# FFN up projections of a two-layer backbone block: seven block products in place of eight, with the activation through DRAM

## The chip, the cores and the metric

The kernel runs on 1 core of one Trainium2 chip. The metric is device microseconds of one execution. The kernel before takes 2263.75 us (median of 3 runs, 2263.47 to 2264.12). The names of the engines are those of the profile: PE is TensorE's matmul, PEld its weight load, DVE is VectorE, ACT is ScalarE, POOL is GpSimd, SP is SyncE, which here issues the DMAs.

## The reference, cut to what matters

1024 tokens of 1024 features go through two layers. Layer 0 has a pooling and attention mixer, layer 1 a token-gating mixer; behind each mixer stands the same FFN, with its own weights (D_FF is 2816, float32 throughout):

```python
def conv_ffn(h, w_up, conv_w, conv_b, w_down):
    hu = h @ w_up                                  # (1024, 1024) @ (1024, 5632)
    hcv = lax.conv_general_dilated(hu, conv_w[:, None, :], window_strides=(1,), padding='SAME',
                                   dimension_numbers=('NWC', 'WIO', 'NWC'),
                                   feature_group_count=hu.shape[-1]) + conv_b
    gate, up = jnp.split(hcv, 2, axis=-1)
    return (jax.nn.silu(gate) * up) @ w_down       # (1024, 2816) @ (2816, 1024)

x = post(x, mixer(pre(x, ...)), g_mix_post, gt_m)      # x + gate * rmsnorm(y)
x = post(x, conv_ffn(pre(x, ...), ...), g_ffn_post, gt_f)
```

The convolution runs over the tokens, three wide, separately for each of the 5632 features.

## The kernel before

**Products.** A float32 matrix is held as the sum of two float32r parts, `hi` (ACT casts it, line 115 for weights) and `lo` (DVE subtracts `hi` from the float32 value, line 52). `three` (lines 121 to 123) forms a product of two such matrices from three matmuls of 128 x 128 by 128 x 512 (hi hi, hi lo, lo hi). `piece` loads 128 x 512 weights (256 KB), casts and subtracts; its tiles come from the pool `wp`, open for the whole program, with 4 raw buffers, so the weights of the next stage can be loaded while the last one still runs.

**Up phase of the FFN.** The features stand on the partitions. There are 44 chunks of 128 output features: chunk f (0 to 21) of the gate and chunk 22 + f of the up half. Each chunk is worked for two halves of 512 tokens (`h[0]`, `h[1]`), over 8 blocks of 128 input features: 44 x 2 x 8 x 3 = 2112 matmuls in a layer. The modulated input of half 1 isn't ready when the phase begins: the mixer's last projection (tiles `e` in layer 0, `o` in layer 1) has just ended, and `tail` (`post`, then `post_pair` for two pairs of token blocks) has to norm it, add the residual, norm again, transpose on PE (tiles `tra`, `trb`) and modulate. So `ffn_order` runs the first 6 chunks (HEAD = 3 pairs) for half 0 alone, then for half 1, and the others for both. Names: `hiha`, `loha` are half 0's input in layer 0, `hihb` and so on those of half 1, `hiu`, `lou` a chunk's weights, `pu` the PSUM bank.

**Activation.** `conv_unit` applies the convolution to the 512 tokens of a bank: ACT's Identity with scale and bias (line 366), two DVE instructions over 511 columns (`stt`, line 49), and some one-column instructions for the seam between the halves. `gated` multiplies. Half 0's activation is split and stays on the chip; half 1's goes to DRAM (`act_d`, 256 KB for each f).

**Down phase.** 22 blocks of the contraction, half by half, 1056 matmuls in a layer (tiles `d`, weights `rawd`, `hid`, `lod`); half 1's activation is read back (`arw`). `post` of the result makes the input of the next mixer (tiles `sv` are its first projection).

**Background.** `ada_block` computes 512 modulation columns: 4 DMAs of 512 KB, 8 DVE instructions of 128 x 512 (`aacc`), a few small ones. Six blocks run in layer 0's up phase, two in layer 1's.

**Order.** A tile framework assigns buffers from pools, adds the semaphore waits, and sets each engine's order by priorities (`tc.high_priority` moves the weights' loads and splits ahead). Each engine runs its instructions in order. A pool that opens where another has closed takes over its space, and waits until the last reader is done.

The listing shows the kernel before, with the lines that the profile names.

## Time and profile before

| | |
|---|---|
| runs of the kernel before | 2263.47, 2263.75, 2264.12 us |
| span of the profiled execution | 2260.8 us |
| span of layer 0's up phase (482.9 to 970.3) | 487.40 us |
| span of layer 1's up phase (1520.3 to 2004.0) | 483.70 us |
| PE busy | 2222.1 us, 98% of the span |
| DVE, ACT, POOL busy | 1336.0, 958.1, 0.2 us |

The profiler gives the span, from the first to the last recorded instruction of one execution; that execution's own device time isn't listed apart from it. The median of the runs is 2.95 us above the span, and this difference is taken as what lies around the span. The mean duration of a matmul of 128 x 512 in the groups is its time from issue to end; neighbours overlap, so what one costs is the distance between two starts. The same holds for DVE: the starts of two neighbours lie a little closer than one lasts.

### The profile page before, as it was taken

Reading aid. Unit: us, or ns where it says so; the run is one execution under the profiler, and the core shown is the slowest. Engines: PE = TensorE matmul, PEld = TensorE weight load, DVE = VectorE, ACT = ScalarE, POOL = GpSimd, SP = SyncE. Lnnn points to the kernel's source line nnn. Section 1 sums busy time; section 2 is a strip of 40 time slices with the busy share of each in tenths; the row PEclk is TensorE's granted clock in tenths of the full one; section 3 lists DMA queues with packets and bytes.
Section 4 is the critical chain, followed back from the end, with each engine's and each line's share of the span. In section 5 each row is a group of like instructions: output and inputs, shape, how many; then the busy total and the mean of one; then the engine's idle time right before and its main releaser. Section 6 shows DMA issues by size and latency. Waiting matters only on the chain.

```text
span 2260.8 us, 27374 instructions
## 1 busy us (share of the span) xinstructions
PE 2222.1 (98%) x9862; PEld 1744.5 (77%) x9862; DVE 1336.0 (59%) x2608; ACT 958.1 (42%) x1766; POOL 0.2 (0%) x4
## 2 busy tenths in 40 slices
PE   6999999999999999999999999999999999999998
PEld 3775455888888888888887888878888888888776
DVE  5686667678875455534625467379655555443555
ACT  5645654465333333324524432266333333323444
POOL 0000000000000000000000000000000000000000
PEclk9999999999999999999999999999999999999999
DMA  8110112554451111225535246246411111124675
GB/s 305 63 43 19 52 47 92 189 200 145 159 168 65 61 61 57 66 89 164 178 97 168 93 132 195 88 166 205 140 65 61 60 63 61 61 80 131 197 246 181
DMA packets 120824, 266.25 MB, mean 118 GB/s; under 512 B 13416, under 2 KB 14056, under 8 KB 120560
## 3 DMA queue, kind: packets, MB, share of 16 engines
q1 hardware_dynamic: 120688, 264.51, 35.9%
q8 instruction: 77, 1.26, 0.2%
q14 instruction: 59, 0.48, 0.1%
HBM read 236.14 MB, written 28.31 MB: 117 GB/s over the span
## 4 chain that ended last, share of the span: by engine, by line
PE 92%; DMA 3%; DVE 2%; ACT 1%; issue 1%; SPq 0%; DVEq 0%; ACTq 0%
PE pu L121 15%; PE pu L122 15%; PE pu L123 15%; PE d L122 6%; PE d L121 6%; PE d L123 6%; PE o L710 3%; PE tr L703 2%; PE o L122 1%; PE o L121 1%; PE sv L121 1%; PE o L123 1%; PE sv L123 1%; PE sv L122 1%; DMA rawd<-in_wdn_dram 1%; PE e L121 1%
## 5 line engine op out<-in xcount | busy, mean ns | idle before, releaser
L49 DVE SCALAR_TENSOR_TENSOR c<-pu,cvw,c 128x511 f32<-128x511 f32 x352 | 263.3, 749 | 214.9 <-ACT c L366 209.7
L52 DVE TENSOR_TENSOR lod<-rawd,hid 128x512 fp32r<-128x512 f32 x220 | 151.5, 691 | 254.7 <-ACT hid L115 252.0
L121 PE MATMUL pu<-hiha,hiu 128*128 128x512 f32 x704 | 274.4, 390 | 0.0
L122 PE MATMUL pu<-loha,hiu 128*128 128x512 f32 x704 | 274.2, 389 | 0.0
L122 PE MATMUL pu<-lohb,hiu 128*128 128x512 f32 x704 | 274.1, 389 | 0.0
L123 PE MATMUL pu<-hiha,lou 128*128 128x512 f32 x704 | 274.1, 389 | 0.0
L123 PE MATMUL pu<-hihb,lou 128*128 128x512 f32 x704 | 274.1, 389 | 0.0
L121 PE MATMUL pu<-hihb,hiu 128*128 128x512 f32 x704 | 274.0, 389 | 0.0
L115 ACT CAST hid<-rawd 128x512 fp32r<-128x512 f32 x220 | 136.6, 622 | 286.8 <-PE d L123 239.7
L115 ACT CAST hiu<-rawu 128x512 fp32r<-128x512 f32 x208 | 129.5, 623 | 283.5 <-PE pu L122 256.2
L52 DVE TENSOR_TENSOR lou<-rawu,hiu 128x512 fp32r<-128x512 f32 x208 | 143.5, 690 | 147.5 <-ACT hiu L115 146.7
L366 ACT ACTIVATE c<-pu,cvw 128x512 f32<-128x512 f32 x176 | 136.5, 777 | 142.8 <-PE pu L123 142.8
L122 PE MATMUL d<-lod,a 128*128 128x512 f32 x448 | 177.8, 397 | 1.3 <-DVE lod L52 1.2
L123 PE MATMUL d<-hid,a 128*128 128x512 f32 x448 | 176.9, 395 | 0.0
L121 PE MATMUL d<-hid,a 128*128 128x512 f32 x448 | 176.6, 396 | 0.0
L123 PEld LDWEIGHTS pu<-hihb,lou 128*128 128x128 f32 x704 | 132.2, 188 | 27.4
L123 PEld LDWEIGHTS pu<-hiha,lou 128*128 128x128 f32 x704 | 132.2, 188 | 27.4
L121 PEld LDWEIGHTS pu<-hihb,hiu 128*128 128x128 f32 x704 | 132.2, 188 | 27.3
L122 PEld LDWEIGHTS pu<-loha,hiu 128*128 128x128 f32 x704 | 132.2, 188 | 27.3
L122 PEld LDWEIGHTS pu<-lohb,hiu 128*128 128x128 f32 x704 | 132.2, 188 | 27.2
L121 PEld LDWEIGHTS pu<-hiha,hiu 128*128 128x128 f32 x704 | 132.2, 188 | 27.1
L49 DVE SCALAR_TENSOR_TENSOR aacc<-ar,silc,aacc 128x512 f32<-128x512 f32 x140 | 104.7, 748 | 15.1 <-DMA ar<-in_wada_b_dram 13.7
(355 smaller groups left out, 3851.2 us busy)
## 6 DMA issues: line engine op xcount, KB each, us to landing
rawd<-in_wdn_dram SPq DMA_DIRECT2D x220, 256.0 KB, 2.7
rawu<-in_wup_dram SPq DMA_DIRECT2D x200, 256.0 KB, 2.6
ar<-in_wada_b_dram SPq DMA_DIRECT2D x80, 512.0 KB, 3.9
actd<-c SPq DMA_DIRECT2D x44, 256.0 KB, 2.0
arw<-actd SPq DMA_DIRECT2D x44, 256.0 KB, 2.9
aw<-in_wada_a_dram SPq DMA_DIRECT2D x16, 512.0 KB, 7.1
rawe<-in_wout_e_dram SPq DMA_DIRECT2D x32, 256.0 KB, 3.0
rawsv<-in_win_v_dram SPq DMA_DIRECT2D x32, 256.0 KB, 2.6
```

The costliest lines, as they stand in the source:

```text
L49: V.scalar_tensor_tensor(out=out, in0=in0, scalar=scalar, in1=in1, op0=op0, op1=op1)
L52: V.tensor_tensor(out=out, in0=in0, in1=in1, op=op)
L115: A.copy(out=hi, in_=raw)
L121: nc.tensor.matmul(ps, a[0], b[0], start=first, stop=False)
L122: nc.tensor.matmul(ps, a[0], b[1], start=False, stop=False)
L123: nc.tensor.matmul(ps, a[1], b[0], start=False, stop=last)
L366: A.activation(out=c, in_=ps, func=AF.Identity, scale=w1, bias=b)
L703: nc.tensor.transpose(out=tr[:, j * P:(j + 1) * P], in_=pr[j][:, c * P:(c + 1) * P], identity=ident)
L710: nc.tensor.matmul(po, vv[:, kb, a], pt, start=c == 0, stop=c == nch - 1)
```

## The change

Take one f. Its gate and up chunks (128 output features each), the two halves of the input features (blocks 0 to 3 and 4 to 7) and the two halves of the tokens form a 2 x 2 by 2 x 2 block product: A11, A12 are the gate chunk's weights for the two halves of the input features, A21, A22 those of the up chunk; B11, B21 are token half 0's input features, B12, B22 those of token half 1. The kernel before does 8 block products, of 12 matmuls each. The changed one does 7, with sums on both sides (Winograd's form of Strassen's scheme):

- weight sums, anew for every f: s1 = A21 + A22, s2 = s1 - A11, s3 = A11 - A21, s4 = A12 - s2 (DVE, 128 x 512 each, float32);
- input sums, once in a layer: t1 = B12 - B11, t2 = B22 - t1, t3 = B22 - B12, t4 = B21 - t2, made by `post_sums` in 8 steps (2 pairs of token blocks, 4 steps `kk` of two feature blocks); in a step ACT runs 7 instructions of 128 x 256, DVE 7, POOL 4;
- products: `stage_a` does A11 B11 (into `x`) and A12 B21 (`y`), `stage_b` s2 t2 (added to `x`), s1 t1 (`z`) and s3 t3 (added to `x`), `stage_c` s4 B22 (added to `z`) and A22 t4 (added to `x`). Between them x, y and z are copied and added into two tiles of 1024 tokens, `c1` (gate) and `c2` (up).

Each of the seven left-hand sides is split into hi and lo (7 ACT casts, 7 DVE subtractions of 128 x 512). The convolution then runs on `c1` and `c2` in SBUF, over 1024 columns at once, without a seam. The whole activation (512 KB for each f) goes to DRAM, and the down phase reads back both halves (`load_acts(0)`, `load_acts(1)`). `stage_a` of the first three f (LEAD = 3), which need half 0 alone, run while half 1 is made. The pool of the weights is now opened and closed by stage: `wp0` (layer 0's mixer), none in an up phase, whose own pool `up0` or `up1` holds its weights, `wd0` (down), `wn0` (layer 1's mixer), `wd1`.

The core of the diff (removed lines that the listing shows are left out, as are the changes to comments):

```diff
-    wp = ctx.enter_context(tc.tile_pool(name="wp", bufs=3))
...
+    def open_wp(es, name):
+        pools["wp"] = es.enter_context(tc.tile_pool(name=name, bufs=3))
...
+    def post_sums(ys, step, nxt, name, h0, b22, ts):
+        l, w = nxt
+        y = ys[0]
+        for pair in range(2):
+            post_pair(y, 1, pair, ys[1], step, None, nxt, f"{name}{pair}", False)
+            tsl = slice(2 * pair * P, 2 * (pair + 1) * P)
+            for kk in range(4):
+                nm = f"{name}{pair}{kk}"
+                ps = bank(f"tr{nm}")
+                for q in range(2):
+                    for i in range(2):
+                        nc.tensor.transpose(out=ps[:, (2 * q + i) * P:(2 * q + i + 1) * P],
+                                            in_=y[:, 2 * pair + i, (kk + 4 * q) * P:(kk + 4 * q + 1) * P],
+                                            identity=ident)
+                full, ta, tb = ntmp("fs" + nm), ntmp("ta" + nm), ntmp("tb" + nm)
+                W = 2 * P
+                for q in range(2):
+                    k = kk + 4 * q
+                    A.activation(out=full[:, q * W:(q + 1) * W], in_=ps[:, q * W:(q + 1) * W], func=AF.Identity,
+                                 scale=gmod[:, l, w, k:k + 1], bias=ada[:, l, 24 * w + k:24 * w + k + 1])
+                b12, f22 = full[:, 0:W], full[:, W:2 * W]
+                t = [ta[:, 0:W], ta[:, W:2 * W], tb[:, 0:W], tb[:, W:2 * W]]
+                h0h, h0l = (x.bitcast(F32) for x in h0)
+                A.copy(out=b22[:, 0, kk, tsl], in_=f22)
+                tt(t[0], b12, h0h[:, kk, tsl], ALU.subtract)
+                tt(t[0], t[0], h0l[:, kk, tsl], ALU.subtract)
+                G.tensor_tensor(out=t[2], in0=f22, in1=b12, op=ALU.subtract)
+                G.tensor_tensor(out=t[1], in0=f22, in1=t[0], op=ALU.subtract)
+                tt(b22[:, 1, kk, tsl], f22, b22.bitcast(F32)[:, 0, kk, tsl], ALU.subtract)
+                tt(t[3], h0h[:, kk + 4, tsl], t[1], ALU.subtract)
+                tt(t[3], t[3], h0l[:, kk + 4, tsl], ALU.add)
+                for i in (0, 2, 1, 3):
+                    A.copy(out=ts[i][:, 0, kk, tsl], in_=t[i])
+                    (G.tensor_tensor if i in (1, 2) else V.tensor_tensor)(
+                        out=ts[i][:, 1, kk, tsl], in0=t[i], in1=ts[i].bitcast(F32)[:, 0, kk, tsl], op=ALU.subtract)
+    LEAD = 3
+    def ffn(l, pu, h0, tail, step, nxt, background=()):
...
+        act_d = dram.tile([NF, P, T], F32, name=f"actd{l}")
...
+            def split(src, name):
+                t = up.tile([P, 2, HT], F32R, tag="hl", name=name, bufs=4)
                 A.copy(out=t[:, 0, :], in_=src)
                 tt(t[:, 1, :], src, t.bitcast(F32)[:, 0, :], ALU.subtract)
+                return t
+            def product(ps, w, b, first):
+                for k in range(4):
+                    ks = slice(k * P, (k + 1) * P)
+                    three(ps, (w[:, 0, ks], w[:, 1, ks]), b(k), first and k == 0, k == 3, not first)
+            def raw_sum(f, name, in0, in1, op):
+                s = up.tile([P, HT], F32, tag="s", name=f"{name}_{l}_{f}", bufs=4)
+                tt(s, in0, in1, op)
+                return s
+            def c_tile(name):
+                return up.tile([P, T], F32, tag="c", name=name, bufs=6)
...
+                o = 2 * (f % 2)
...
+                with tc.high_priority():
+                    for i in range(2):
+                        nc.sync.dma_start(out=ring[f][i], in_=wup[l, f + i * NF])
+            def stage_a(f):
+                nm = f"{l}_{f}"
+                ws = []
+                if f >= LEAD:
+                    load(f)
+                for i in range(2):
+                    with tc.high_priority():
+                        if f >= LEAD:
+                            raw = ring[f][0][:, halves(i)]
+                        else:
+                            raw = up.tile([P, HT], F32, tag="ra", name=f"ra{nm}_{i}", bufs=2)
+                            nc.sync.dma_start(out=raw, in_=wup[l, f][:, halves(i)])
+                        ws.append(split(raw, f"wa{nm}_{i}"))
+                x = chain[f] = pu(f"x{nm}")
+                c1 = c1s[f] = c_tile(f"c1{nm}")
+                product(x, ws[0], lambda k: (h0[0][:, k, :], h0[1][:, k, :]), True)
+                A.copy(out=c1[:, 0:HT], in_=x)
+                y = bank(f"y{nm}")
+                product(y, ws[1], lambda k: (h0[0][:, 4 + k, :], h0[1][:, 4 + k, :]), True)
+                tt(c1[:, 0:HT], y, c1[:, 0:HT], ALU.add)
+            def stage_b(f):
+                nm = f"{l}_{f}"
+                if f < LEAD:
+                    load(f)
+                g, u = ring[f]
+                x, c1 = chain[f], c1s[f]
+                with tc.high_priority():
+                    a11, a12, a21, a22 = g[:, 0:HT], g[:, HT:T], u[:, 0:HT], u[:, HT:T]
+                    s1 = raw_sum(f, "s1", a21, a22, ALU.add)
+                    s2 = raw_sum(f, "s2", s1, a11, ALU.subtract)
+                    w2 = split(s2, f"w2{nm}")
+                    w1 = split(s1, f"w1{nm}")
+                    s3 = raw_sum(f, "s3", a11, a21, ALU.subtract)
+                    w3 = split(s3, f"w3{nm}")
+                product(x, w2, ops["t2"], False)
+                A.copy(out=c1[:, HT:T], in_=x)
+                z = bank(f"z{nm}")
+                product(z, w1, ops["t1"], True)
+                c2 = c_tile(f"c2{nm}")
+                A.copy(out=c2[:, HT:T], in_=z)
+                product(x, w3, ops["t3"], False)
+                tt(c2[:, HT:T], x, c2[:, HT:T], ALU.add)
+                return f, z, c2, s2, a12, a22
+            def conv(f, up_, c, name):
+                fc = f + NF * up_
                 w0, w1, w2, b = (cvw[:, t * 44 + fc:t * 44 + fc + 1] for t in range(4))
+                a = c_tile(name)
+                A.activation(out=a, in_=c, func=AF.Identity, scale=w1, bias=b)
+                stt(a[:, 1:T], c[:, 0:T - 1], w0, a[:, 1:T], ALU.mult, ALU.add)
+                stt(a[:, 0:T - 1], c[:, 1:T], w2, a[:, 0:T - 1], ALU.mult, ALU.add)
+                return a
+            def stage_c(f, z, c2, s2, a12, a22):
+                nm = f"{l}_{f}"
+                x, c1 = chain.pop(f), c1s.pop(f)
+                with tc.high_priority():
+                    s4 = raw_sum(f, "s4", a12, s2, ALU.subtract)
+                    w4 = split(s4, f"w4{nm}")
+                    w22 = split(a22, f"wd{nm}")
+                product(z, w4, ops["b22"], False)
+                tt(c1[:, HT:T], z, c1[:, HT:T], ALU.add)
+                product(x, w22, ops["t4"], False)
+                A.copy(out=c2[:, 0:HT], in_=x)
+                g = conv(f, 0, c1, f"ag{nm}")
                 A.activation(out=g, in_=g, func=AF.Silu)
+                u = conv(f, 1, c2, f"au{nm}")
                 tt(g, g, u, ALU.mult)
+                nc.sync.dma_start(out=act_d[f], in_=g)
+            for f in range(LEAD):
+                stage_a(f)
...
+            tail(b22, ts)
...
+            late = None
+            for f in range(NF):
+                b = stage_b(f)
+                if late:
+                    stage_c(*late)
+                late = b
+                if f >= LEAD - 1:
+                    if f + 1 < NF:
+                        stage_a(f + 1)
+                    stage_c(*late)
+                    late = None
+                if f > 4 and background:
+                    ada_block(background.pop(0))
...
+        open_wp(es, f"wd{l}")
...
+        def load_acts(hf):
             for f in range(NF):
+                raw = ntmp(f"arw{l}_{f}_{hf}")[:, :HT]
+                nc.sync.dma_start(out=raw, in_=act_d[f][:, halves(hf)])
+                t = act[f] = new_act(f, hf)
+                A.copy(out=t[:, 0, :], in_=raw)
+                tt(t[:, 1, :], raw, t.bitcast(F32)[:, 0, :], ALU.subtract)
...
+        load_acts(0)
+        ys = back_proj(pu, acts, lambda k: wdn[l, k], NF, 0, step, f"d{l}")
+        load_acts(1)
+        h0 = post(ys, 0, step, nxt, f"f{l}0")
+        if nxt is not None:
...
+            es.close()
+            es = ExitStack()
+            open_wp(es, f"wn{l}")
+            return h0, ys, es
...
```

**PE where layer 0's up phase begins.** Before, the first chunk's matmuls follow the mixer's last ones (`e`), and the transposes `tra` of the first pair come amid the matmuls of chunk 1; a row with x3 stands for three instructions:

```order
1752 L122 MATMUL pu0_22_0_4193<-hiha0_3541,hiu02201_4189 128x512
1753 L123 MATMUL pu0_22_0_4193<-hiha0_3541,lou02201_4190 128x512
1754 L121 MATMUL pu0_1_0_4241<-hiha0_3541,hiu0100_4231 128x512
1755 L295 MATMUL tra100_4042<-ident_83,ye1_3677 128x128
1756 L295 MATMUL tra101_4052<-ident_83,ye1_3677 128x128
1757 L295 MATMUL tra102_4062<-ident_83,ye1_3677 128x128
1758 L122 MATMUL pu0_1_0_4241<-loha0_3542,hiu0100_4231 128x512
1759 L295 MATMUL tra100_4042<-ident_83,ye1_3677 128x128 x3
```

Of the change, the end of `stage_a` of f = 2 (tile `y0_2`), the transposes of both pairs (`tra100` to `tra113`), and the first matmul of `stage_b` of f = 0:

```order
1777 L128 MATMUL y0_2_4102<-hiha0_3542,wa0_2_1_4084 128x512
1778 L342 MATMUL tra100_4148<-ident_80,ye1_3678 128x128 x4
1779 L342 MATMUL tra101_4174<-ident_80,ye1_3678 128x128 x4
1780 L342 MATMUL tra102_4200<-ident_80,ye1_3678 128x128 x4
1781 L342 MATMUL tra103_4226<-ident_80,ye1_3678 128x128 x4
1782 L342 MATMUL tra110_4279<-ident_80,ye1_3678 128x128 x4
1783 L342 MATMUL tra111_4305<-ident_80,ye1_3678 128x128 x4
1784 L342 MATMUL tra112_4331<-ident_80,ye1_3678 128x128 x4
1785 L342 MATMUL tra113_4357<-ident_80,ye1_3678 128x128 x4
1786 L126 MATMUL x0_0_4009<-t2_0_4118,w20_0_4390 128x512
```

All transposes of half 1 now stand behind the 72 matmuls of the three `stage_a`, and no product stands between them and the first that needs t2.

**SP where layer 0's down phase begins.** Before, the down weights (`rawd`) are issued between the last up weights and the stores of the activation (`actd`):

```order
277 L112 DMA rawu04300_7814<-in_wup_dram 128x512
278 L384 DMA actd0_4004<-c0_19_1_7488 128x512
279 L112 DMA rawu04301_7820<-in_wup_dram 128x512
280 L112 DMA rawd00000_7905<-in_wdn_dram 128x512
281 L112 DMA rawd00001_7923<-in_wdn_dram 128x512
282 L112 DMA rawd00002_7941<-in_wdn_dram 128x512
283 L384 DMA actd0_4004<-c0_20_1_7648 128x512
```

Of the change (`ag0_21` is the activation of the last f):

```order
205 L418 DMA raw_0_4383<-in_wup_dram 128x1024
206 L490 DMA actd0_3993<-ag0_19_7219 128x1024
207 L490 DMA actd0_3993<-ag0_20_7357 128x1024
208 L490 DMA actd0_3993<-ag0_21_7458 128x1024
209 L117 DMA rawd00000_7586<-in_wdn_dram 128x512
210 L117 DMA rawd00001_7604<-in_wdn_dram 128x512
```

The first down weights now stand behind the store of the last activation, and by the waits of the built program they wait for that store to be complete, since their pool takes the space of the up phase's.

## Rows read from the trace of the kernel before

**Rows 1.** The page: busy time, share of the span, instructions

```profile
PE 2222.1 (98%) x9862; PEld 1744.5 (77%) x9862; DVE 1336.0 (59%) x2608; ACT 958.1 (42%) x1766; POOL 0.2 (0%) x4
```

**Rows 2.** The chain that ended last, by engine and by line

```profile
PE 92%; DMA 3%; DVE 2%; ACT 1%; issue 1%; SPq 0%; DVEq 0%; ACTq 0%
PE pu L121 15%; PE pu L122 15%; PE pu L123 15%; PE d L122 6%; PE d L121 6%; PE d L123 6%; PE o L710 3%; PE tr L703 2%; PE o L122 1%; PE o L121 1%; PE sv L121 1%; PE o L123 1%; PE sv L123 1%; PE sv L122 1%; DMA rawd<-in_wdn_dram 1%; PE e L121 1%
```

**Rows 3.** Stretches: length, busy us and instructions per engine, granted clock, DMA share, GB/s

```profile
core 0: us, PE busy (x) PEld busy (x) DVE busy (x) ACT busy (x) POOL busy (x), PEclk, DMA share, GB/s
29.20:33.30 4.10, 4.04 (x10) 3.14 (x11) 3.95 (x9) 3.21 (x8) 0.00 (x0) 0.50 0.51 204
33.30:37.40 4.10, 4.10 (x18) 1.79 (x16) 2.28 (x6) 1.32 (x2) 0.00 (x0) 0.97 0.00 0
...
510.00:540.00 30.00, 30.00 (x134) 24.79 (x133) 29.71 (x62) 17.21 (x30) 0.00 (x0) 1.00 0.45 142
...
482.90:970.30 487.40, 487.40 (x2181) 403.66 (x2180) 309.69 (x655) 189.14 (x334) 0.00 (x0) 1.00 0.32 105
1520.30:2004.00 483.70, 483.70 (x2149) 400.25 (x2149) 289.83 (x618) 189.19 (x333) 0.00 (x0) 1.00 0.27 88
```

**Rows 4.** PE's timeline at three seams: start, duration, line, operation, tiles

```profile
482.56 0.39 PE L123 MATMUL e<-hie,lox 128*128 128x512 f32 x1
482.79 0.39 PE L121 MATMUL pu<-hiha,hiu 128*128 128x512 f32 x1
...
970.09 0.40 PE L123 MATMUL pu<-hiha,lou 128*128 128x512 f32 x1
970.33 0.39 PE L121 MATMUL d<-hid,a 128*128 128x512 f32 x1
...
1218.62 0.39 PE L123 MATMUL d<-hid,ah 128*128 128x512 f32 x1
1218.94 1.02 PE L767 MATMUL rw<-ws,ones 128*1 128x512 f32 x2
```

**Rows 5.** DVE by line and form: busy us, mean ns, idle before and its releasers

```profile
L49 DVE SCALAR_TENSOR_TENSOR c<-pu,cvw,c 128x511 f32<-128x511 f32 x352 | 263.3, 749 | 214.9 <-ACT c L366 209.7
L52 DVE TENSOR_TENSOR lou<-rawu,hiu 128x512 fp32r<-128x512 f32 x208 | 143.5, 690 | 147.5 <-ACT hiu L115 146.7
L49 DVE SCALAR_TENSOR_TENSOR aacc<-ar,silc,aacc 128x512 f32<-128x512 f32 x140 | 104.7, 748 | 15.1 <-DMA ar<-in_wada_b_dram 13.7
...
L49 DVE SCALAR_TENSOR_TENSOR yd<-yd,rpf,xinf 128x1024 f32<-128x1024 f32 x16 | 20.2, 1281 | 2.5 <-DMA xinf<-x3d 2.4
```

**Rows 6.** DVE's timeline just after the first up matmul of layer 0

```profile
483.13 0.69 DVE L52 TENSOR_TENSOR ye<-e,grow 128x512 f32<-128x512 f32 x1
483.74 0.68 DVE L52 TENSOR_TENSOR lou<-rawu,hiu 128x512 fp32r<-128x512 f32 x1
```

**Rows 7.** ACT by line and form, columns as for DVE

```profile
L115 ACT CAST hiu<-rawu 128x512 fp32r<-128x512 f32 x208 | 129.5, 623 | 283.5 <-PE pu L122 256.2 <-issue 12.9 <-PE pq L122 4.8
...
L708 ACT COPY pt<-tr 128x512 f32<-128x512 f32 x44 | 25.5, 584 | 24.0 <-PE tr L703 23.6
...
L159 ACT ACTIVATE junk<-ye 128x1024 bf16<-128x1024 f32 x8 | 8.4, 1055 | 2.7 <-DVE ye L49 2.6
...
L262 ACT ACTIVATE fuf<-trf,ada,gmod 128x256 f32<-128x256 f32 x16 | 8.2, 564 | 2.4 <-PE trf L295 2.4
```

**Rows 8.** DMA issues: tiles, engine, operation and count, KB each, median us to landing

```profile
rawu<-in_wup_dram SPq DMA_DIRECT2D x200, 256.0 KB, 2.6
ar<-in_wada_b_dram SPq DMA_DIRECT2D x80, 512.0 KB, 3.9
actd<-c SPq DMA_DIRECT2D x44, 256.0 KB, 2.0
...
x1d<-ye SPq DMA_DIRECT2D x8, 512.0 KB, 2.9
```

More of the change, by code (lines that the diff above doesn't have):

```diff
@@ L24 @@
 EPS = 1e-6
-HEAD = 3
 _COLS = {}
@@ L117, in piece, with three @@
         return hi, lo
-    def three(ps, a, b, first, last):
-        nc.tensor.matmul(ps, a[0], b[0], start=first, stop=False)
-        nc.tensor.matmul(ps, a[0], b[1], start=False, stop=False)
-        nc.tensor.matmul(ps, a[1], b[0], start=False, stop=last)
+    def three(ps, a, b, first, last, more=False):
+        nc.tensor.matmul(ps, a[0], b[0], start=first, stop=False, skip_group_check=more)
+        nc.tensor.matmul(ps, a[0], b[1], start=False, stop=False, skip_group_check=more)
+        nc.tensor.matmul(ps, a[1], b[0], start=False, stop=last, skip_group_check=more)
     def chunk_weights(src, name, ahead=True):
@@ L318, in post @@
         return h
-    def ffn_order(l):
-        head = [fc for f in range(HEAD) for fc in (f, NF + f)]
-        order = [(fc, (0,)) for fc in head] + [(fc, (1,)) for fc in head]
-        return order + [(fc, (0, 1)) for f in range(HEAD, NF) for fc in (f, NF + f)]
-    def ffn_weights(l, step):
-        fc, hfs = ffn_order(l)[step]
-        return chunk_weights(wup[l, fc], f"u{l}{fc}{hfs[0]}")
-    def ffn(l, pu, h0, first, tail, step, nxt, background=()):
-        act_d = dram.tile([NF, P, HT], F32, name=f"actd{l}")
+    def post_sums(ys, step, nxt, name, h0, b22, ts):
[33 more added lines that the diff above has]
+                        out=ts[i][:, 1, kk, tsl], in0=t[i], in1=ts[i].bitcast(F32)[:, 0, kk, tsl], op=ALU.subtract)
@@ L391, in ffn @@
-            background = list(background)
-            for i, (fc, hfs) in enumerate(ffn_order(l)):
-                w = first[i] if i < len(first) else ffn_weights(l, i)
-                for hf in hfs:
-                    conv_unit(fc, hf, w)
-                if fc >= NF:
-                    for hf in hfs:
-                        gated(fc - NF, hf)
-                    if i > 4 * HEAD and background:
-                        ada_block(background.pop(0))
-            assert not background
-            def acts(f):
-                return act[f][:, 0, :], act[f][:, 1, :]
@@ new lines, in ffn @@
+        load_acts(1)
+        h0 = post(ys, 0, step, nxt, f"f{l}0")
+        if nxt is not None:
+            ys = back_proj(pu, acts, lambda k: wdn[l, k], NF, 1, step, f"d{l}")
+            es.close()
+            es = ExitStack()
+            open_wp(es, f"wn{l}")
+            return h0, ys, es
+        y = slot([P, 4, D], F32, f"yd{l}1")
+        for pair in range(2):
+            ys = back_proj(pu, acts, lambda k: wdn[l, k], NF, 1, step, f"d{l}", (2 * pair, 2 * pair + 1), y)
+            post_pair(y, 1, pair, ys[1], step, None, None, f"f{l}1{pair}")
@@ L750, in hybrid_block @@
         ys = back_proj(pu, mix(1), lambda k: wout_e[k], KC, 1, 0, "e")
[L752 to L753 removed]
+    h0, ys, down = ffn(0, pu, h0, lambda b22, ts: post_sums(ys, 0, (0, 1), "a1", h0, b22, ts), 1, (1, 0), range(6, 12))
     with ExitStack() as es:
+        es.enter_context(down)
         cs = es.enter_context(tc.tile_pool(name="cs", bufs=1))
```

102 lines of the change are left out of this document (39 added, 63 removed).

## The prediction

> **What bounds the kernel now.** I read the page's busy times first: PE works 98% of the span, DVE 59%, ACT 42%, and POOL does nothing [rows 1]. The chain of waits says the same from the end: 92% of it is PE, 45% the three matmuls of the up projections alone [rows 2]. Then I cut out the two up phases: PE is busy in all of 487.40 and 483.70 us at a granted clock of 1.00, while DVE works 309.69 and 289.83 us and ACT 189 [rows 3]. In one stretch of 30 us DVE is busy for 29.71, and PE still loses nothing [rows 3]. Last the seams: where the mixer ends and the up projections begin, the starts lie 0.23 us apart (482.56, 482.79); from up to down 0.24 us (970.09, 970.33); from down to the next mixer 0.32 us [rows 4]. So the kernel is one unbroken row of matmuls. A change has to be counted twice: matmuls that go, and holes that come.
>
> **What goes.** One of eight block products: 22 f x 12 matmuls x 2 layers = 528. An up phase holds 2112 block matmuls and some 70 small ones (the counts 2181 and 2149 show it [rows 3]); these 69 and 37 (transposes of 128 columns, modulation sums) I put at 0.1 us each, under half of a 512-column start distance. (487.40 - 6.9)/2112 = 0.2275, (483.70 - 3.7)/2112 = 0.2273. At 0.2274 the saving is 528 x 0.2274 = 120.1 us.
>
> **The start of an up phase (both layers).** The weights' pool now opens in the up phase, in space that the mixer's pool leaves, so the first load waits for the last matmul of the mixer; call its end 0. Load 2.6 [rows 8] with 0.3 to issue, cast 0.62 [rows 7]: 3.5. The subtraction behind it stands on DVE after two residual instructions of 1024 columns, 1.28 each [rows 5], which follow the mixer's last evacuation; I put PE's steady run at 5.7. Three stage_a are 72 matmuls, 16.4 us. After such a hole the clock is low: the first rows of the trace show 10 matmuls in 4.10 us at a granted clock of 0.50 (1.2 GHz), and 18 in the next 4.10 us at 0.97 (2.4 GHz) [rows 3], which is 8 matmuls, about 2 us, for a restart. So stage_a ends near 24.
>
> Only then come the transposes of half 1, and the eight steps that make B22 and t1 to t4. A step takes three of the four temporary buffers, so it overlaps the next one little. Its chain: Identity over 256 columns 0.56 [rows 7], two DVE subtractions of 256 columns, one on POOL, two on DVE, a cast, a subtraction. A DVE instruction of 256 columns isn't in my rows; half of that of 512 is 0.35 [rows 5], half of the cast 0.31. POOL has no row of arithmetic at all. The nearest is the same operation on DVE: 0.35 if POOL were as fast; the upper end I take from DVE's 1.28 for four times the columns [rows 5]. Between them I take 0.69, DVE's time for twice the columns. The chain is then 0.56 + 0.70 + 0.69 + 0.70 + 0.31 + 0.35 = 3.3, with hand-offs 3.7. ACT's seven instructions are a floor: 2 x 0.56 + 5 x 0.31 = 2.7. Four POOL instructions at 1.28 would be a ceiling of 5.1. I take the middle of 2.7 and 3.7: 3.2. Eight steps are 25.6 us; s1, s2, the cast and the subtraction for the first t2 product, with hand-offs, 3.5. The products go on at 24 + 25.6 + 3.5 = 53. In that time PE has done 16.4 us of matmuls and 3.5 of transposes, work that stays; 33 are lost, and 2 more for the restart: 35 a layer, 70 in all. By the bounds (2.7 and 5.1 a step) it is 62 to 100; if the holes cost no clock, some 8 less.
>
> The row that bears on POOL is only its 0.2 us of busy time [rows 1]. The Trainium skill (GPSIMD Engine Reference, section 3.1, Elementwise) lists a float32 tensor_tensor of 2048 columns at 4497 ns against 2293 on VectorE; by that ratio of two my estimate is 0.7 and the sum stays. Its section 8, Key points, also says that GpSimd shares its SBUF interfaces with VectorE and contends with VectorE instructions that have two SBUF inputs; nearly all of a step's are such, so by that rule the first rival below would come in. No run here shows it yet.
>
> **From up to down (both layers).** Before, the down weights were loaded ahead. Now their pool waits for the last store of the activation. From the last up matmul: copy out of PSUM 0.58, Identity over 1024 columns 1.06 [rows 7], two convolution instructions of 1.28 and a product of about the same, 3.8 [rows 5], the store of 512 KB 2.9 as for x1d (256 KB took 2.0), the weights' load 2.6 [rows 8] with 0.3, a cast 0.62, hand-offs 0.5: 12.4, and 2 for the clock. 14.4 a layer, 29 in all. Without the clock's share 25; with a store of 3.9, the slowest row of that size, and a second load queued before it, 36.
>
> **From down to layer 1's mixer.** Another pool opens: 0.3 + 2.6 + 0.62 and the clock's 2, 5.5 us. Bounds 3 and 8. Layer 1's down phase ends the program as before.
>
> **DVE within the up phase.** Per f it gets 4 weight sums, 7 splits and 3 additions of 512 columns, 4 convolution instructions of 1023 and a product of 1024. Neighbours' starts lie 0.61 apart for 512 columns [rows 6], so 14 x 0.61 + 5 x 1.23 = 14.7 us, against 84 x 0.2274 = 19.1 on PE: without background work DVE has room. A modulation block adds 8 instructions, seven of 0.75 [rows 5], about 5.4 in distance of starts, with its small ones up to 7.4: 20 to 22 in these f. Six blocks in layer 0, two in layer 1, and the catching up after the start: I take 9 and 3.5, 12.5. Bounds: 2, if the slack of the next f takes it up; 25, if every block holds PE up fully. The convolution over 1024 columns saves the seam's small instructions, which were hidden. The extra traffic (22 x 256 KB more stored and read a layer) has room: the DMAs are busy for a third of the stretch [rows 3].
>
> **The sum**, against the profiled span of 2260.8: -120.1 + 70 + 29 + 5.5 + 12.5 = -3.1, 2257.7. The median of the runs is 2.95 above the span: 2260.7, say 2261. The saving and the holes cancel within what I can estimate.
>
> **The rivals.**
> First, slower: the eight steps hang on POOL. Mechanism: four POOL instructions a step, two of them in the chain, in turn with DVE's two-input ones, on the path that PE waits for. From 0.9 us each (4 x 0.9 = 3.6) it decides the sign; at 1.28 a step is 5.1, (5.1 - 3.2) x 8 = 15 a layer, 30 in all: 2291. For it: no row shows POOL doing this, and the order leaves PE nothing else. Against: half of the work of a step is elsewhere.
>
> Second, faster: steps overlap better than I think and run at ACT's 2.7 (-8), DVE's slack takes the modulation blocks (-10), and the restarts cost little (seven are in the sum at 2 us each, -10): 2261 - 28 = 2233. For it: PE lost nothing where DVE was 99% busy [rows 3]. Against: the restart in the first rows shows the low clock, and a chain of 3.3 us can't run at 2.7 with buffers for one and a third steps unless its links are shorter than half of the longer rows.
>
> Third, slower: DVE binds the up phase. Each split waits in DVE's queue behind convolutions of 2 x 1.28, which wait for ACT; only four split buffers lie between, some 11 us of matmuls. If an f takes 20.5 us in place of 19.1, 1.4 x 38 f = 53: 2314. Against it: 14.7 of 19.1.
>
> Fourth, the change does nearly all that the count says: the framework fills the holes (transposes earlier, other buffers) and some 40 us of them remain: 2183. The built order speaks against it: no product stands between stage_a and the tail.
>
> **How the numbers follow.** Forecast 0.45, with its own range of 2249 to 2273; the rivals 0.20, 0.25, 0.07, 0.03. No change that can be measured is within 0.2% of 2263.75, 2259.2 to 2268.3; of the forecast's 0.45 I put 0.18 below it, 0.19 in it and 0.08 above. Faster: 0.18 + 0.25 + 0.03 = 0.46. Same: 0.19. Slower: 0.08 + 0.20 + 0.07 = 0.35. The range takes in the first two rivals with some room, 2225 to 2293, and leaves out the others and their surroundings.
>
> **What would show it.** Each up phase has a hole on PE between the transposes and x's t2 product, 29 us long, and one of 5 us ahead of it; from up to down 12; ahead of sv 4; the granted clock falls to 0.50 behind them. POOL's rows of 128 x 256 read 0.7. Between the holes matmuls start every 0.227 us and from the mixer's last matmul to the first down matmul an up phase takes about 487 - 60 + 35 + 9 + 14 = 485 us in layer 0, near what it took before. The forecast is wrong if POOL's rows read 0.9 or more, if PE waits for DVE inside the steady f, or if the holes are under 20 us.

## The result and the profile after

The changed kernel takes 2276.57 us (median of four runs, 2274.03 to 2279.70), the kernel before on the same chip 2263.61: a ratio of 1.0059, interval 1.0044 to 1.0073. It is slower by 0.6%. The range held it; the likeliest case, 2261, and the sign did not. The profiled execution has a span of 2272.9 us against 2260.8, so 12.1 us are to be found.

The page's busy times and its chain by engine, columns as in [rows 1, 2]:

```profile
PE 2125.0 (93%) x9334; PEld 1655.1 (73%) x9334; DVE 1561.1 (69%) x2444; ACT 1089.0 (48%) x1906; POOL 53.5 (2%) x68
PE 76%; DVE 10%; DMA 6%; issue 4%; ACT 3%; SPq 0%; POOL 0%; DVEq 0%; ACTq 0%; POOLq 0%
```

PE has 528 matmuls fewer and 97 us less to do, and stands still for 148 us where it stood for 39. The chain, 92% PE before, now holds DVE with 10% and DMA with 6%. POOL's 53.5 us look like nothing; the rest of this section is about what they do.

I cut both traces at the same events: the end of the mixer's last matmul (its start and 0.23 us), the first down matmul, the first sv matmul.

| Stretch | before us | after us | difference |
|---|---|---|---|
| to the end of layer 0's mixer | 482.79 | 482.59 | -0.2 |
| up phase, layer 0, to the first down matmul | 487.54 | 494.75 | +7.2 |
| down phase, layer 0, to the first sv | 249.56 | 253.32 | +3.8 |
| mixer, layer 1 | 300.46 | 294.87 | -5.6 |
| up phase, layer 1 | 483.70 | 486.74 | +3.0 |
| down phase, layer 1 | 247.80 | 251.63 | +3.8 |

The seams of [rows 4] in PE's timeline of the kernel after, with the idle time before each row and its releaser in brackets:

```profile
482.36 0.39 PE L128 MATMUL e<-hie,lox 128*128 128x512 f32 x1
487.40 0.73 PE L126 MATMUL x<-hiha,wa 128*128 128x512 f32 x1 [4.66 <-ACT wa L391]
...
526.20 1.12 PE L342 MATMUL tra<-ident,ye 128*128 128x128 f32 x4 [3.48 <-ACT fsa L349]
...
547.40 0.80 PE L126 MATMUL x<-t,w 128*128 128x512 f32 x1 [20.09 <-ACT w L391]
...
977.34 0.79 PE L126 MATMUL d<-hid,a 128*128 128x512 f32 x1 [12.51 <-DMA rawd<-in_wdn_dram]
```

The predicted holes stand where the prediction put them, though the one of 29 us comes in two parts: 13.2 us of waits among the transposes and 20.1 behind them. The one of 12.5 us has its size, but the first t2 product comes 547.40 - 482.59 = 64.81 us after the mixer's end (63.31 in layer 1), not 53. The stretches around it, columns as in [rows 3]:

```profile
core 0: us, PE busy (x) PEld busy (x) DVE busy (x) ACT busy (x) POOL busy (x), PEclk, DMA share, GB/s
482.70:547.40 64.70, 26.30 (x105) 19.66 (x105) 54.37 (x93) 33.88 (x83) 26.66 (x32) 0.70 0.35 123
547.40:552.00 4.60, 4.60 (x10) 3.27 (x11) 4.60 (x9) 1.61 (x3) 0.00 (x0) 0.50 0.02 4
552.00:600.00 48.00, 48.00 (x210) 39.17 (x210) 38.84 (x54) 24.26 (x36) 0.00 (x0) 1.00 0.42 142
```

In the first stretch PE works 26.30 of 64.70 us and DVE 54.37: the steps below show that DVE is what the products wait for. After the hole the clock is at 0.50 (1.2 GHz) for 4.6 us; then PE runs without a gap. Now one step of the input sums, first in DVE's and then in POOL's timeline:

```profile
517.53 0.41 DVE L51 TENSOR_TENSOR tba<-tba,loha 128x256 f32<-128x256 f32 x1
517.87 0.94 DVE L51 TENSOR_TENSOR taa<-fsa,hiha 128x256 f32<-128x256 f32 x1
518.84 0.42 DVE L51 TENSOR_TENSOR taa<-taa,loha 128x256 f32<-128x256 f32 x1
519.19 0.42 DVE L364 TENSOR_TENSOR t<-tba,t 128x256 fp32r<-128x256 f32 x1
519.52 0.95 DVE L51 TENSOR_TENSOR b<-fsa,b 128x256 fp32r<-128x256 f32 x1
520.39 0.94 DVE L51 TENSOR_TENSOR tba<-hiha,taa 128x256 f32<-128x256 f32 x1
521.26 0.94 DVE L364 TENSOR_TENSOR t<-taa,t 128x256 fp32r<-128x256 f32 x1
522.12 0.41 DVE L51 TENSOR_TENSOR tba<-tba,loha 128x256 f32<-128x256 f32 x1
```

```profile
517.78 0.75 POOL L357 TENSOR_TENSOR tba<-fsa 128x256 f32<-128x256 f32 x1 [0.46 <-DVE t L364]
519.35 0.84 POOL L358 TENSOR_TENSOR taa<-fsa,taa 128x256 f32<-128x256 f32 x1 [0.82 <-DVE taa L51]
520.15 0.91 POOL L364 TENSOR_TENSOR t<-tba,t 128x256 fp32r<-128x256 f32 x1
521.02 0.90 POOL L364 TENSOR_TENSOR t<-taa,t 128x256 fp32r<-128x256 f32 x1
```

The same operation of the same size takes DVE 0.41 or 0.94 us. Lay the starts side by side: it is 0.94 exactly where it starts while a POOL row runs. Where POOL's starts second (517.78 beside DVE's 517.53, 519.35 beside 519.19), DVE's keeps its 0.41. In both layers all 62 that start while a POOL row runs take 0.86 to 0.96 us, and the 58 others 0.41 to 0.43. Between starts a long one is 0.87 in place of 0.34, so a step is 4 x 0.87 + 3 x 0.34 = 4.5; from 517.53 to 522.12 it took 4.59. DVE never pauses in it. The products of t2 are released by the cast of a weight sum, which stands on DVE behind the last step. POOL's four instructions cost DVE 4 x 0.53 = 2.1 us a step; done on DVE they would cost it 4 x 0.34 = 1.4.

### The profile page after: what moved, and what is told of

Its sections match the earlier page's. It is cut to its first block, busy times and chain, and to the rows that moved or that the text cites. A ratio compares the mean times of both kernels' runs of the same rounds, so it can differ in the third digit from the quotient of the medians.

```text
span 2272.9 us, 26115 instructions
## 1 busy us (share of the span) xinstructions
PE 2125.0 (93%) x9334; PEld 1655.1 (73%) x9334; DVE 1561.1 (69%) x2444; ACT 1089.0 (48%) x1906; POOL 53.5 (2%) x68
## 4 chain that ended last, share of the span: by engine, by line
PE 76%; DVE 10%; DMA 6%; issue 4%; ACT 3%; SPq 0%; POOL 0%; DVEq 0%; ACTq 0%; POOLq 0%
PE x L126 6%; PE x L128 6%; PE x L127 6%; PE d L127 5%; PE d L128 5%; PE d L126 5%; PE o L848 3%; PE z L126 3%; PE z L128 3%; PE z L127 3%; DMA arw<-actd 2%; PE tr L841 2%; DMA rawd<-in_wdn_dram 1%; PE y L126 1%; PE y L128 1%
## 5 line engine op out<-in xcount | busy, mean ns | idle before, releaser
L391 ACT CAST w<-s 128x512 fp32r<-128x512 f32 x176 | 108.8, 623 | 271.4 <-PE z L128 110.7
L126 PE MATMUL x<-t,w 128*128 128x512 f32 x352 | 141.0, 401 | 40.7 <-ACT w L391 40.2
L51 DVE TENSOR_TENSOR w<-s,w 128x512 fp32r<-128x512 f32 x176 | 120.1, 686 | 50.0 <-ACT w L391 49.4
L128 PE MATMUL x<-t,w 128*128 128x512 f32 x352 | 139.9, 398 | 0.0
L127 PE MATMUL x<-t,w 128*128 128x512 f32 x352 | 138.7, 394 | 0.0
L126 PEld LDWEIGHTS d<-hid,a 128*128 128x128 f32 x448 | 85.2, 190 | 49.2 <-ACT hid L120 30.7
L48 DVE SCALAR_TENSOR_TENSOR ag<-c,cvw,ag 128x1023 f32<-128x1023 f32 x88 | 112.8, 1282 | 10.0 <-ACT ag L470 9.1
L48 DVE SCALAR_TENSOR_TENSOR au<-c,cvw,au 128x1023 f32<-128x1023 f32 x88 | 112.8, 1281 | 1.2 <-ACT au L470 0.2
L126 PEld LDWEIGHTS x<-t,w 128*128 128x128 f32 x352 | 67.2, 191 | 56.0 <-ACT w L391 41.0
L127 PEld LDWEIGHTS d<-lod,a 128*128 128x128 f32 x448 | 85.0, 190 | 24.6 <-DVE lod L51 7.3
L127 PE MATMUL d<-lod,ah 128*128 128x512 f32 x256 | 99.8, 390 | 0.9 <-DVE lod L51 0.9
L128 PE MATMUL d<-hid,ah 128*128 128x512 f32 x256 | 99.6, 389 | 0.0
L126 PE MATMUL d<-hid,ah 128*128 128x512 f32 x256 | 99.6, 389 | 0.0
L128 PEld LDWEIGHTS d<-hid,a 128*128 128x128 f32 x448 | 85.1, 190 | 17.3
```

The costliest lines, as they stand in the source:

```text
L48: V.scalar_tensor_tensor(out=out, in0=in0, scalar=scalar, in1=in1, op0=op0, op1=op1)
L51: V.tensor_tensor(out=out, in0=in0, in1=in1, op=op)
L126: nc.tensor.matmul(ps, a[0], b[0], start=first, stop=False, skip_group_check=more)
L127: nc.tensor.matmul(ps, a[0], b[1], start=False, stop=False, skip_group_check=more)
L128: nc.tensor.matmul(ps, a[1], b[0], start=False, stop=last, skip_group_check=more)
L391: A.copy(out=t[:, 0, :], in_=src)
```

## The experiments

Each ratio is to the kernel before as measured beside that run; it stood between 2261.58 and 2263.61 us, so a difference to the changed kernel's 2276.57 is good to about 2 us.

My theory after the result: POOL's instructions and DVE's two-input ones hold each other up, which makes a step 4.6 us. The rivals: the order of the work (the tail behind stage_a), the pools, PE's clock, and the address of operands.

**The sums on DVE alone.**

```diff
-                G.tensor_tensor(out=t[2], in0=f22, in1=b12, op=ALU.subtract)
-                G.tensor_tensor(out=t[1], in0=f22, in1=t[0], op=ALU.subtract)
+                tt(t[2], f22, b12, ALU.subtract)
+                tt(t[1], f22, t[0], ALU.subtract)
...
-                    (G.tensor_tensor if i in (1, 2) else V.tensor_tensor)(
-                        out=ts[i][:, 1, kk, tsl], in0=t[i], in1=ts[i].bitcast(F32)[:, 0, kk, tsl], op=ALU.subtract)
+                    tt(ts[i][:, 1, kk, tsl], t[i], ts[i].bitcast(F32)[:, 0, kk, tsl], ALU.subtract)
```

> The four POOL instructions of each step of the input sums go to DVE; nothing else changes. Theory (turns): a POOL and a DVE instruction with two SBUF inputs each run in turns, so DVE's 0.41 us becomes 0.94; without POOL a step is 11 DVE instructions at 0.34 between starts, 3.75 us in place of 4.6, the first product with t2 starts some 58 us after the mixer's end in place of 64.8, and the kernel gains 2 x 6.8 = 13.6 us: about 2263. Rival (these DVE instructions are long by themselves, POOL is only slow): DVE gets four more long ones, 4.6 + 4 x 0.34 to 0.87 = 6 to 8 us a step, 2297 or more.

Measured: 2257.64 us, ratio 0.9979 (0.9970 to 0.9988): faster than the kernel before, 18.9 us under the changed kernel. One step in DVE's timeline:

```profile
515.73 0.43 DVE L51 TENSOR_TENSOR taa<-fsa,taa 128x256 f32<-128x256 f32 x1
516.06 0.43 DVE L51 TENSOR_TENSOR b<-fsa,b 128x256 fp32r<-128x256 f32 x1
516.40 0.43 DVE L51 TENSOR_TENSOR tba<-hiha,taa 128x256 f32<-128x256 f32 x1
...
519.41 0.43 DVE L51 TENSOR_TENSOR taa<-fsa,taa 128x256 f32<-128x256 f32 x1
```

Eleven instructions now fill a step of 3.68 us (515.73 to 519.41), shorter than seven did beside POOL: 8 x 0.92 = 7.4 us a layer. The first t2 product comes at 50.3 and 50.8 after the mixers' ends, 14.5 and 12.5 us earlier. That is more than the steps give, since DVE's order now lets it go with about two steps still to do; the kernel gains 18.9 us, not 27. I had expected 13.6.

**The tail ahead of stage_a, and both edits together.**

```diff
-            for f in range(LEAD):
-                stage_a(f)
...
             tail(b22, ts)
+            for f in range(LEAD):
+                stage_a(f)
```

> The sums of half 1 are emitted ahead of the three stage_a, so the transposes of pair 0 come amid their matmuls, as before; POOL stays. Theory (the steps are a chain that starts 13 us later than it need): the steps start about 12 us after the mixer's end in place of 25.5, pair 1's residual and norm then share DVE with them (+5), and the first t2 product starts at about 57 in place of 64.8: 2 x 8 us less, about 2260. Rival (DVE is full there anyway): the chain only moves in pieces, no change, 2273 to 2277.

> Both edits: the sums wholly on DVE, emitted ahead of stage_a. Theory (turns, and late start): steps of 3.75 us from about 12, with pair 1's residual and norm between them: first t2 product at about 50 us after the mixer's end, 2 x 15 us less, about 2247. Rival (one of the two was no cause): only the other's gain, about 2261.

Measured: 2261.12 us, ratio 0.9995 (0.9986 to 1.0005), and 2251.92, 0.9953 (0.9941 to 0.9966). The t2 product comes at 56.8 and 57.0 in the first, at 48.9 and 49.4 in both together, as expected, though the time with both is 5 us above the 2247 expected. PE's waits for the norm and for the first t2 weights from 482 to 600 us (total, times, longest), first with the tail moved alone, then with both edits:

```profile
PE tra L342 <- DVE ye L293: 9.4, 1, 9.4
...
PE x L126 <- ACT w L391: 3.8, 1, 3.8
```

```profile
PE tra L342 <- DVE ye L293: 14.7, 2, 14.5
...
PE x L126 <- ACT w L390: 1.1, 1, 1.1
```

The long wait ahead of the products is gone, but another has come: the transposes of the second pair wait for its norm, which stands on DVE behind the first pair's steps. Order gives 15 us with POOL and, without it, 6, which fits DVE's amount of work on this path as the limit.

**The convolution's tiles in a pool of their own**, so that the down weights' space is free when the last product is done, not when the last activation is stored. The last four of the activation's tiles move to a second pool, `aq`.

```diff
+            cv = es.enter_context(tc.tile_pool(name=f"cv{l}", bufs=1))
...
-                return up.tile([P, T], F32, tag="c", name=name, bufs=6)
+                return cv.tile([P, T], F32, tag="c", name=name, bufs=6)
...
-        ap = es.enter_context(tc.tile_pool(name=f"act{l}", bufs=14))
+        ap = es.enter_context(tc.tile_pool(name=f"act{l}", bufs=10))
+        aq = es.enter_context(tc.tile_pool(name=f"acq{l}", bufs=4))
...
```

> The 1024-token tiles of the convolution get a pool of their own, so the down weights' pool takes space that is free after the last up product and doesn't wait for the last store of the activation. Theory (the hole from up to down is the chain of last convolution, store and load): the hole falls from 12.6 us to about 4.5 (issue 0.3, load 2.6, cast 0.62, and a subtraction behind the last convolution on DVE), 2 x 8 us less and a little of the clock: about 2259. Rival (the last convolution on DVE and ACT holds the first splits back anyway): hole of 10 or more, 2 x 2.5 at most, 2271 or more.

Measured: 2252.25 us, ratio 0.9954 (0.9942 to 0.9966). PE's wait ahead of the first down product, 900 to 1000 us:

```profile
PE d L126 <- ACT hid L120: 4.1, 1, 4.1
```

The hole shrank from 12.6 to 4.1 as expected. The total, 24.3 us less, is 7 more than the 17 of the holes. Some of the rest is in the steady up phase; PE from 800 to 900 us, of the changed kernel and then with the new pool (columns as in [rows 3]):

```profile
800.00:900.00 100.00, 100.00 (x438) 82.00 (x437) 78.99 (x99) 51.01 (x75) 0.00 (x0) 1.00 0.23 79
```

```profile
800.00:900.00 100.00, 100.00 (x443) 82.83 (x442) 79.19 (x100) 52.07 (x76) 0.00 (x0) 1.00 0.23 79
```

Its matmuls start 0.2268 us apart in place of 0.2290, in both layers. That is worth some 8 us (0.0022 for each of 3696 matmuls); other waits take part of it back, and the two up phases are 3.1 us shorter in the profiled executions.

**POOL beside DVE, measured apart.** 160 subtractions on POOL, on scratch tiles that nothing reads, run beside layer 0's down phase; layer 1's is the control.

```diff
+        if l == 0:
+            scr = ap.tile([P, 3, 256], F32, name="scr", bufs=1)
+            G.memset(scr, 1.0)
+            for i in range(160):
+                G.tensor_tensor(out=scr[:, 2, :], in0=scr[:, 0, :], in1=scr[:, 1, :], op=ALU.subtract)
```

> In layer 0's down phase POOL gets 160 subtractions of 128 x 256 on a scratch tile that nothing else reads or writes; DVE's and PE's work stays, and layer 1's down phase has none, as a control. Theory (turns): with DVE idle one takes about 0.6 us (0.87 less DVE's 0.28 of the turn); beside a DVE instruction with two SBUF inputs both are longer, POOL about 0.9, DVE's subtraction of 512 columns about 1.2 in place of 0.69; DVE's instructions with one SBUF input stay as they are. Rival (POOL takes 0.86 by itself, and DVE's length has another reason): 0.86 always, DVE's durations as in layer 1. The time hardly moves by either, PE being the bound there: 2274 to 2284.

DVE by form in layer 0's stretch with POOL (985 to 1145 us), columns as in [rows 5], and one POOL row with no DVE instruction beside it:

```profile
L51 DVE TENSOR_TENSOR lod<-rawd,hid 128x512 fp32r<-128x512 f32 x53 | 55.4, 1053 | 33.8 <-ACT hid L120 33.7
L51 DVE TENSOR_TENSOR a<-arw,a 128x512 fp32r<-128x512 f32 x24 | 28.0, 1177 | 2.0 <-ACT a L534 2.0
...
L48 DVE SCALAR_TENSOR_TENSOR yd<-yd,rpf,xinf 128x1024 f32<-128x1024 f32 x4 | 6.9, 1732 | 0.0
L51 DVE TENSOR_TENSOR yd<-d,grow 128x512 f32<-128x512 f32 x8 | 5.3, 681 | 0.0
...
L293 DVE TENSOR_SCALAR yd<-yd,rnf 128x1024 f32<-128x1024 f32 x3 | 3.3, 1087 | 0.0
...
1054.35 0.73 POOL L544 TENSOR_TENSOR scr<-scr 128x256 f32<-128x256 f32 x1
```

And in layer 1's (2030 to 2200 us):

```profile
L51 DVE TENSOR_TENSOR lod<-rawd,hid 128x512 fp32r<-128x512 f32 x73 | 49.7, 689 | 62.9 <-ACT hid L120 62.7
L51 DVE TENSOR_TENSOR a<-arw,a 128x512 fp32r<-128x512 f32 x28 | 19.0, 687 | 9.4 <-ACT a L534 9.3
...
L51 DVE TENSOR_TENSOR yd<-d,grow 128x512 f32<-128x512 f32 x10 | 6.9, 688 | 0.2
L48 DVE SCALAR_TENSOR_TENSOR yd<-yd,rpf,xinf 128x1024 f32<-128x1024 f32 x4 | 5.1, 1283 | 2.0 <-DMA xinf<-x3d 2.0
```

This settles the mechanism. Instructions with two inputs from SBUF go from 0.69 to 1.05 and 1.18, and from 1.28 to 1.73; the product that reads d from PSUM stays at 0.68. POOL takes 0.73 to 0.74 in the 14 of its 160 that no DVE instruction runs beside, and 0.98 on average over all. POOL's instruction reads two operands from SBUF, and a DVE instruction that does so too takes turns with it. The TENSOR_SCALAR with one input can be held up too (0.75 in the kernel with the sums on DVE; here 1.22, 0.74 and 1.30). The Trainium skill (GPSIMD Engine Reference, section 8, Key points) names two SBUF inputs as such a case, and the trace agrees. The Trainium skill (SBUF — State Buffer, section SBUF: two separate sides) says that one of the two engines holds the shared ports for a whole instruction and the other is fully blocked. By that, I estimate, a pair would need 0.34 + 0.73 = 1.07 us; 0.87 was measured, so here some of it overlaps. I had also expected that the time would stay at 2274 to 2284; it was 2294.49 in its one run. In that down phase PE waited 6.1 us for the down weights' low parts, in 8 times, and 7.8 us for the norm ahead of the transposes `trf`.

**The clock.** 126 matmuls a layer, whose result nothing reads, in the first two holes of the changed kernel's up phases.

```diff
+        idle = mbank("idle" + name)
...
+                nc.tensor.matmul(idle, h0[0][:, 0, 0:P], h0[0][:, 0, :], start=True, stop=True)
...
+                keep_busy(84 if (pair, kk) == (1, 3) else 14 if pair else 0)
```

> The changed kernel with 126 matmuls more in each up phase's two first holes (into a bank that nothing reads), placed where PE only waits. Theory (the low clock behind a hole is a cost of its own): the granted clock stays up, the first 72 products and the first ones with t2 start 0.227 us apart and not 0.427, some 4 us a layer, about 2269. Rival (DVE sets the end of the hole and the phase behind it, PE catches up anyway): no change or the fillers' own delay, 2276 to 2280.

Measured: 2277.92 us, ratio 1.0066 (1.0053 to 1.0079), as without them. PE behind the first hole without the filling, and then, with it, in the first hole and the stretches that answer to those after (columns as in [rows 3]):

```profile
487.40:492.00 4.60, 4.19 (x9) 2.90 (x10) 3.01 (x10) 3.05 (x7) 0.00 (x0) 0.51 0.97 295
```

```profile
482.20:507.00 24.80, 24.75 (x116) 19.84 (x115) 18.65 (x37) 13.86 (x31) 1.64 (x2) 1.00 0.68 236
...
543.60:548.00 4.40, 4.37 (x10) 3.04 (x11) 4.40 (x8) 1.64 (x3) 0.00 (x0) 0.50 0.01 4
552.00:600.00 48.00, 45.53 (x190) 36.28 (x189) 35.85 (x49) 21.87 (x33) 0.00 (x0) 0.96 0.41 132
```

Some of the filling ran in the first hole: the clock stayed at 1.00 and the t2 product came 3.3 us earlier (61.5). But PE then lost 2.5 of 48 us, and the up phase ended 482.30 us after the mixer's end, without the filling 482.09; in layer 1 it ended 3.3 us later than without. What PE gained it gave back: those 2.5 us are one wait for ACT's copy into c, so PE isn't what sets the pace there. The filling ended 4.6 us too soon for the second hole, so what that restart costs was not tried.

**The address of operands.** In the changed kernel layer 1's mixer is 5.6 us shorter between the cuts, though nothing of it was changed. Of these, 2.0 are work on the other side of the cut: two `rw` and eight `sb` matmuls that stood behind the first sv product now stand ahead of it, where PE waits for the weights:

```profile
1227.88 1.15 PE L910 MATMUL sb<-rows,lnb 2*128 2x128 f32 x8 [0.66 <-ACT rows L906]
1229.71 1.02 PE L905 MATMUL rw<-ws,ones 128*1 128x512 f32 x2 [0.68 <-DMA rawsv<-in_win_v_dram]
```

For the rest, the addresses: the activation's and the mixer's tiles had moved by 32 bytes. Once the changed kernel gets the old offset, once the kernel before the new one, each by a tile of eight numbers that nothing reads.

```diff
         ap = es.enter_context(tc.tile_pool(name=f"act{l}", bufs=14))
+        pad = ap.tile([P, 8], F32, name="pad", bufs=1)
+        V.memset(pad, 0.0)
```

```diff
+    V.memset(sm.tile([P, 8], F32, name="pad", bufs=1), 0.0)
```

> The changed kernel with the on-chip activation's tiles moved by 32 bytes in SBUF (addresses of 32 modulo 64, as before the change; 0 modulo 64 in the changed kernel). A matmul of the down phase that reads such a tile as its stationary operand starts 0.2330 us after the last one in the kernel before and 0.2272 in the changed one. Theory (the address is the cause): 0.233 again, 672 matmuls a phase x 0.0058 x 2 = 8 us more, about 2284. Rival (it comes from what else runs there, such as the reloading of half 0): 0.2272, no change, 2276.

> The kernel before, with one 32-byte tile more among the small ones, so that the on-chip activation (56 tiles) and seven of the eight tiles of layer 1's mixer output (m) lie at addresses of 0 modulo 64 in place of 32. Theory (a stationary operand at 32 modulo 64 costs 0.006 us a matmul): 2 x 672 matmuls of the down phases and some 340 of the mixer's last projection, 0.0058 each, 9.8 us less, about 2252. Rival (the start distances of 0.233 in the kernel before come from something else that the change removed): no change, 2262.

Measured: 2281.48 us, ratio 1.0085 (1.0069 to 1.0101), 4.9 above the changed kernel; and 2254.23, 0.9965 (0.9952 to 0.9979), 7.8 under the kernel before. PE's products that have the tile a as the stationary operand (the 128 x 128 block that PEld loads), in layer 0's down phase (columns as in [rows 5]): first with the old offset, then of the changed kernel.

```profile
L128 PE MATMUL d<-hid,a 128*128 128x512 f32 x223 | 89.0, 399 | 0.0
```

```profile
L128 PE MATMUL d<-hid,a 128*128 128x512 f32 x217 | 84.7, 390 | 0.0
```

Their starts lie 0.2332 apart in the one and 0.2272 in the other. The time lies between the two expectations, and the intervals of the two ratios overlap, so the distances show the effect and the time hardly does; in layer 1's down phase PE's waits are 3.1 us shorter with the old offset, which takes some of it back. The kernel before and then the same with its tile of 32 bytes, PE in the same 30 us of the down phase (length, busy us and instructions, granted clock, DMA share, GB/s):

```profile
973.00:1003.00 30.00, 30.00 (x130) 1.00 0.32 105
```

```profile
973.00:1003.00 30.00, 30.00 (x132) 1.00 0.32 104
```

Two matmuls more in the same time, at the same clock and the same traffic. The new offset is not all of it: the products with lod still start 0.232 apart there (0.235 before), and layer 1's mixer is 2.2 us shorter by it. So part of the time of the changed kernel is a gain by accident, which an edit that moves tiles can give or take.

**All repairs.** The sums on DVE, the norms of both pairs ahead of all steps, the first chunk ahead of the tail and the others behind it, the pool of the convolution, and the first weights loaded into the steps' buffers, which don't wait for the mixer; and the same without the last of these.

```diff
         for pair in range(2):
             post_pair(y, 1, pair, ys[1], step, None, nxt, f"{name}{pair}", False)
+        for pair in range(2):
...
+                            if f == 0:
+                                raw = ntmp(f"ra{nm}_{i}")[:, :HT]
...
-            for f in range(LEAD):
-                stage_a(f)
+            stage_a(0)
...
             tail(b22, ts)
+            for f in range(1, LEAD):
+                stage_a(f)
```

> The changed kernel with five edits: sums on DVE; both pairs' residuals and norms emitted ahead of all steps; the whole of it emitted after the first stage_a and ahead of the other two; a pool of its own for the convolution's tiles; the first two raw weight tiles of an up phase in buffers that no stage's pool has to leave. Theory (the loss of the change lies in the two seams): first t2 product at about 42 us after the mixer's end in place of 64.8 and 63.3, up to down 4 in place of 12.6, some 5 us of the clock: 2276.6 - 44 - 17 - 5 = 2210. Rival (DVE's total work in the hole sets its end, whatever the order, as e3 against e1 suggests): t2 at 48 or later, 2225 or more.

> The same without the last edit: the first raw weights wait for the mixer's pool again. Theory: the hole ahead of stage_a is 4.7 us in place of about 1, but the first t2 product doesn't hang on it: 2 us or less between the two kernels, about 2211. Rival (the early start moves the whole phase): 2 x 3.5 us more than with it, about 2217.

Measured: **2211.06 us, ratio 0.9776 (0.9764 to 0.9789)**, and 2218.50, 0.9807 (0.9789 to 0.9824). The first is 50.5 us faster than the kernel before beside it (2261.58). Its busy times, and PE's waits from 482 to 1000 us:

```profile
PE 2118.1 (96%) x9334; PEld 1652.7 (75%) x9334; DVE 1543.7 (70%) x2508; ACT 1083.2 (49%) x1906; POOL 0.2 (0%) x4
```

```profile
PE tra L343 <- DVE ye L293: 6.3, 2, 5.1
PE tra L343 <- ACT fsa L350: 5.9, 2, 3.0
PE ab L252 <- DVE aacc L48: 4.5, 4, 2.0
PE d L126 <- ACT hid L120: 3.9, 1, 3.9
...
```

Where the changed kernel waited 20.1 and 12.5 us, no wait is above 5.1. The t2 product comes at 42.5 in both layers. The early load of the first weights was expected to be worth 2 us or less and is worth 7.4, as its rival said: without it the t2 product comes at 44.6 and 45.1, and layer 1's up phase is 3.3 us longer. Where the rest comes from was not traced.

## Why the prediction was wrong

The step that failed is the start of the up phase, in its size of a step of the input sums: "I take the middle of 2.7 and 3.7: 3.2". It was 4.6, and the products went on at 64.8 and 63.3 where the sum put 53. The hole and its place were right. I had costed the chain of a step by its links and each link by how long its instruction runs alone; but DVE was full, and each POOL instruction lengthened one of DVE's. The first rival, at 2291, named the mechanism ("in turn with DVE's two-input ones") and priced another, POOL's own speed: "From 0.9 us each (4 x 0.9 = 3.6) it decides the sign". POOL's groups of rows average 0.77 to 0.91, so by that point alone it was a draw; the bill was DVE's. The experiment with the sums on DVE confirms it from the other side: without POOL the kernel is at 2257.6, faster than before.

The terms, both layers, in us; the measured ones are differences in the profiled executions:

| Term | predicted | measured |
|---|---|---|
| start of the up phases | 70 | 92.9 (47.2 + 45.7) |
| up to down | 29 | 30 (holes 12.66, 12.57 and the restarts) |
| down to mixer | 5.5 | 3.5 |
| DVE in the steady up phase | 12.5 | 3 to 4 |
| waits for down weights, layer 1 | none | 3.5 |
| starts further apart in the steady up phase | none | 8.2 |
| what is left in the down phases and layer 1's mixer | none | -10 |

The first is 64.81 and 63.31, less 16.4 for stage_a and 3.5 for the transposes, plus 2.3 each for the restart (4.6 us at 0.50 for 10 matmuls of 0.227). The differences add up to 22.9 + 1 - 2 - 8.5 + 3.5 + 8.2 - 10 = 15.1, and -3.1 + 15.1 = 12.0, against 12.1. That it closes is in part by construction: the -10 is 5.6 of the mixer, read from the table of stretches, and about 4.4 of the down phases, which is what their other terms leave over. 2.0 of the mixer's 5.6 are the matmuls ahead of the cut, which the row "down to mixer" holds; the experiment with the old offset gave 4.9 for the activation's tiles. The range held the time partly by luck: what the sum had too low or lacked comes to 35.6, what it had too high or lacked the other way to 20.5.

- **The matmuls that go: right.** 9862 - 9334 = 528. But those that stay in the steady up phase start 0.2290 apart, not 0.2267. Those with wd as the stationary operand, or a low part as the moving one, start 0.226 to 0.228 apart, the others 0.229 to 0.233, and with the convolution's pool it is 0.2268, in the kernel with all repairs 0.2269; the sums on DVE and the order left it at 0.2290. So it goes with the pool, which moves the up phase's tiles. That points to where operands lie; no run moved them alone, and the cause stays open.
- **From up to down: right**, link by link, and the experiment with the convolution's pool took out what the prediction said it consists of.
- **DVE in the up phase: too high.** The slack of the next f takes up most modulation blocks; PE's waits for the sum aacc come to 2.4 us in layer 0. The third rival (2314) is out, and so is the fourth (2183): nothing filled the holes of itself.
- **The second rival (2233)** had DVE's slack right, and the steps wrong.

## What to carry to other kernels

Work moved to another engine has two prices: its own time there, and what it adds to the instructions beside it; look up the operands of what will run beside it before taking a duration from a row measured alone. When a change takes matmuls out of an unbroken row of matmuls, cost the holes first: here the same seven products were worth +13 or -51 us by the order, the pools and one engine's choice around them. And before crediting a small difference to an edit, look whether stretches that it doesn't touch have moved too.
